# Output projection of the attention taken by halves of the positions, with the first half's norm inside it, and SBUF pools on two sides

## The chip, the cores and the metric

The kernel runs on one core of a Trainium2 chip. The metric is the device time of one execution in microseconds (us), lower is better; the median of three executions of the kernel before is 2689.87 us (2687.54 to 2693.98).

## The reference

A trunk of two layers over one sequence: S = 1024 positions, D = 1024 features, float32 throughout. The part that matters here is the end of layer 0's attention, its gated residual, and the start of the feed-forward network (FFN) behind it. `y` is the attention of all 16 heads times a sigmoid gate, before the output projection.

```python
# attention: 16 heads of 64, causal, a decay from a forget gate on the logits
    y = (att * sigmoid(o))                 # (S, D)
    x = x + g1 * (y @ w_out)               # output projection, gated residual
    h = rmsnorm(x, norm2_g) * (1 + sc2) + sh2
    a = h @ w_up                           # FFN up-projection, D x 5632
    a = causal_depthwise_conv3(a)          # over positions
    g, val = split(a)
    x = x + g2 * ((silu(g) * val) @ w_down)
```

Layer 1 replaces the attention by a spatial gating unit (SGU), and has an FFN too. `c` gives all shifts, scales and gates.

## The kernel before, in words

**Products.** A float32 product is made of three matmuls of halves: `pair` (L121) splits an operand into a rounded high part (a cast on ACT, L126) and the rest (a subtraction on DVE, L119), and `mm3` (called at L104) multiplies high by high, high by low and low by high. A "step" below is one such group of three 128x512 matmuls: one block of 128 features of `y` against one block of 128 output features, for a half (512) of the positions.

**Order.** All PE instructions of this part run in the order in which they are written (the chain in `mm`, as long as `inorder` is set). The order on DVE, ACT and on SP's DMA queue is made by a scheduler from the same program.

**The attention** goes through eight pairs of heads, p = 0 to 7. While the softmax of one pair keeps DVE and ACT busy, a second stream of work (`stream`) gives PE something to do: `tick(w)` takes steps from it at a rate (`rate`) per unit of attention work. For p = 1 to 7 the stream holds the input projection of the next pair. When the last projection is done, the stream goes on, at rate 1.4, with two things:

- `x_transposed`: the residual x is loaded (512 KB tiles), transposed by PE (16 groups of four 128x128 transposes, L157) and copied out of PSUM by ACT (L883) into eight tiles `xt[k, half]`, features on partitions;
- `out_early`: the output projection for pairs 0 to 5. For each of the eight output blocks m and both halves it makes the steps for p = 0 to 3, adds them to x with the gate (`axpy`, on DVE, L855), and then the same for p = 4 and 5. The operands `w` (blocks of w_out) and `y` are loaded as 256 KB pieces into a ring of two buffers `fraw` (L835) and split by `pair`.

**The tail.** When the attention has ended, the steps of p = 6 and 7 follow for both halves, 96 matmuls, and the last of these write the banks that the FFN will use (`bankX`, `bankY`).

**Between attention and FFN.** `arena` then opens the pool in which the FFN's operands live, on the memory that the attention's pools gave back. `operands1` makes the first operands from the first half of the positions: it writes x to DRAM (`spill`, L1108), squares it (ACT, L1085) and adds the squares (DVE, L1039) into one tile, sums that tile over the partitions with four one-column matmuls, takes the inverse root, spreads it over the partitions with a broadcast matmul (`norm_t`), multiplies (DVE, L1039) and modulates x (`scale`, ACT, L1073), and splits the result into high and low tiles `hc` (`put_op`; ACT L1026, DVE L1039). They are named B11 and B21 after the place they take in the FFN's blocked product. `square_half` (L1098) squares the second half, `start_up` loads and splits the FFN's first weights (`rw`, `ow`), and `next_operands` norms the second half within the FFN's first product, at hooks behind the 7th and 14th group of matmuls.

```python
                self.rate = 1.4
                yield from x_transposed()
                yield from out_early()
        ...
        self.fox()
        self.arena()
        s02 = self.ada_scale(0, 2)
        for _ in self.operands1(s02):
            pass
```

## Time and profile before

The profiled execution took 2692.37 us, 1.77 us of them outside the span of its engines.

| what | value |
|---|---|
| median of three runs | 2689.87 us |
| profiled execution, span | 2692.37 us, 2690.6 us |
| mean granted PE clock | 0.977 |
| PE busy, matmuls | 2563.3 us (95%), 12522 |
| DVE, ACT, POOL busy | 78%, 54%, 6% |
| attention's output projection begins in PE's stream | about 668 us |
| last matmul of the output projection issued | 802 us |
| first FFN matmuls in an unbroken row | from about 828 us |

How to read it: times are in us from the start of the span. A row of the timeline gives start, duration, engine, line, operation, output and inputs; in brackets stands how long the engine had been idle and which instruction on another engine released it. Matmuls overlap in the array, so the end of one row lies behind the start of the next; the distance between starts is what a matmul costs. "PEld" is the loading of a matmul's stationary operand. A row of the groups gives the busy time of all instructions of one form, the mean of one in ns, and the idle time ahead of them.

### The profile page before, as it was taken

To read this page: it belongs to the slowest core of one execution; us is meant where nothing else is said; L and a number is where in the kernel's file an instruction comes from. 1 tells how busy PE (TensorE), PEld (TensorE's weight loads), DVE (VectorE), ACT (ScalarE), POOL (GpSimd) and SP (SyncE) were. 2 spreads that over 40 slices of the span, in tenths; PEclk is the share of its full clock that TensorE was granted. 3 is DMA by queue.
4 is the path that set the end of the run, shared out by engine and by line. 5 is a ranking of instruction groups with operands and counts; after the bars stand their busy time and mean duration, and the time that the engine had idled before them with its cause. 6 is when DMAs were issued, how large, how long until landed. Compare 5 with 4: busy or idle time off the path is not lost.

```text
span 2690.6 us, 35246 instructions
## 1 busy us (share of the span) xinstructions
PE 2563.3 (95%) x12522; PEld 2179.0 (81%) x12522; DVE 2096.8 (78%) x3630; ACT 1458.9 (54%) x2310; POOL 173.7 (6%) x289
## 2 busy tenths in 40 slices
PE   6999999998997899999999999999998999999997
PEld 5988889898776688788888888888876888888886
DVE  7678777887768888898688766666888888877875
ACT  7347766777635454455446544654465555555444
POOL 1122222222200000000000000000000000000000
PEclk9999998998998999999999999999999999999999
DMA  6751111113222344545745346557452343337562
GB/s 232 245 172 56 56 54 54 56 52 118 74 85 62 115 128 149 170 137 198 252 159 178 98 154 194 186 180 278 157 174 73 102 149 114 118 102 287 161 197 90
DMA packets 315512, 377.61 MB, mean 140 GB/s; under 512 B 18760, under 2 KB 196040, under 8 KB 315336
## 3 DMA queue, kind: packets, MB, share of 16 engines
q1 hardware_dynamic: 315112, 375.30, 42.6%
q8 instruction: 98, 1.61, 0.2%
q14 instruction: 78, 0.64, 0.1%
q10 hardware_dynamic: 224, 0.06, 0.0%
HBM read 285.57 MB, written 89.72 MB: 139 GB/s over the span
## 4 chain that ended last, share of the span: by engine, by line
PE 80%; DVE 10%; ACT 5%; issue 2%; DMA 2%; POOL 0%; SPq 0%; DVEq 0%; ACTq 0%; POOLq 0%
PE bankX L104 20%; PE banka L104 18%; PE bankY L104 17%; PE pj L104 7%; PE ms L104 5%; PE o L104 3%; PE op L104 3%; PE s L104 2%; PE ms L157 2%; PE pv L104 2%; DVE hc L1039 1%; DVE ow L1039 1%; DVE x L1039 1%; PE ms L1645 1%; DVE x L1524 1%
## 5 line engine op out<-in xcount | busy, mean ns | idle before, releaser
L1026 ACT CAST ow<-rw 128x1024 fp32r<-128x1024 f32 (+1 forms) x438 | 398.7, 911 | 472.1 <-PE bankX L104 157.8
L1039 DVE TENSOR_TENSOR ow<-rw,ow 128x1024 fp32r<-128x1024 f32 (+1 forms) x438 | 457.9, 1046 | 172.7 <-ACT ow L1026 171.0
L104 PE MATMUL bankX<-hc,ow 128*128 128x512 f32 x1920 | 470.8, 393 | 18.0 <-DVE ow L1039 10.1
L104 PEld LDWEIGHTS bankX<-hc,ow 128*128 128x128 f32 x1920 | 361.2, 189 | 95.7 <-DVE ow L1039 11.6
L104 PE MATMUL banka<-hc,ow 128*128 128x512 f32 x1608 | 392.9, 393 | 6.5 <-ACT hc L1026 2.8
L104 PE MATMUL bankY<-hc,ow 128*128 128x512 f32 x1584 | 388.2, 392 | 0.8 <-DVE ow L1039 0.8
L104 PEld LDWEIGHTS banka<-hc,ow 128*128 128x128 f32 x1608 | 301.2, 189 | 71.3 <-ACT hc L1026 4.4
L104 PEld LDWEIGHTS bankY<-hc,ow 128*128 128x128 f32 x1584 | 296.0, 188 | 64.1 <-issue 1.9
L104 PE MATMUL pj<-x,h 128*128 128x384 f32 (+1 forms) x1536 | 315.5, 347 | 0.3 <-DVE x L119 0.3
L104 PEld LDWEIGHTS pj<-x,h 128*128 128x128 f32 x1536 | 271.3, 192 | 4.9 <-DVE x L119 0.5
L1524 DVE SCALAR_TENSOR_TENSOR x<-x,prm,x 128x1023 f32<-128x1023 f32 (+1 forms) x160 | 204.3, 1279 | 2.8 <-ACT x L1522 2.3
L104 PE MATMUL bankY<-ow 128*128 128x512 f32 x720 | 204.0, 391 | 0.2 <-DVE x L1043 0.2
L104 PE MATMUL banka<-ow 128*128 128x512 f32 x672 | 187.3, 391 | 0.5 <-DVE x L1043 0.5
L104 PEld LDWEIGHTS bankY<-ow 128*128 128x128 f32 x720 | 135.5, 189 | 28.7 <-DVE x L1043 0.6
L104 PE MATMUL bankX<-ow 128*128 128x512 f32 x588 | 156.1, 392 | 0.0
L104 PEld LDWEIGHTS banka<-ow 128*128 128x128 f32 x672 | 125.8, 188 | 27.3 <-ACT x L1073 0.9
L104 PE MATMUL ms<-ow 128*128 128x512 f32 x546 | 139.9, 390 | 0.9 <-DVE pp L1039 0.9
L104 PE MATMUL pv<-pt,w 128*128 128x256 f32 (+1 forms) x640 | 118.2, 293 | 14.0 <-ACT pt L782 11.4
L104 PEld LDWEIGHTS bankX<-ow 128*128 128x128 f32 x588 | 110.7, 188 | 23.5 <-issue 0.5
L119 DVE TENSOR_TENSOR pt<-ms,pt 128x512 fp32r<-128x512 f32 (+1 forms) x160 | 100.3, 632 | 29.6 <-ACT pt L782 28.1
L782 ACT CAST pt<-ms 128x512 fp32r<-128x512 f32 (+1 forms) x160 | 85.3, 539 | 67.3 <-PE ms L157 62.9
L104 PEld LDWEIGHTS ms<-ow 128*128 128x128 f32 x546 | 102.0, 188 | 23.7 <-DVE pp L1039 2.8
(293 smaller groups left out, 3884.8 us busy)
## 6 DMA issues: line engine op xcount, KB each, us to landing
rw<-yd SPq DMA_DIRECT2D x210, 256.0 KB
rw<-in_ffn_w_up_dram SPq DMA_DIRECT2D x88, 512.0 KB
yd<-pp SPq DMA_DIRECT2D x60, 512.0 KB
rw<-in_ada_w_dram SPq DMA_DIRECT2D x48, 512.0 KB
rw<-in_ffn_w_down_dram SPq DMA_DIRECT2D x88, 256.0 KB
rw<-in_sgu_w_in_dram SPq DMA_DIRECT2D x32, 512.0 KB
yd<-x SPq DMA_DIRECT2D x30, 512.0 KB
fraw<-in_fox_w_in_dram SPq DMA_DIRECT2D x96, 128.0 KB
```

The source lines that it names most:

```text
L104: i = self.nc.tensor.matmul(out, lhsT, rhs, start=start, stop=stop, skip_group_check=self.strict)
L119: return (eng or self.nc.vector).tensor_tensor(lo, full, hi.bitcast(F32), op=ALU.subtract)
L157: i = self.nc.tensor.transpose(ps[: s.shape[1], j * P : (j + 1) * P], s, self.ident)
L782: nc.scalar.copy(pt[:, 0, :nb], ps[:, :nb])
L1026: return self.ao(self.nc.scalar.copy(t[:, 0], src))
L1039: return self.vo(self.nc.vector.tensor_tensor(out, a, b, op=op))
L1524: stt(o[:, j:], a[:, : S - j], w[2 - j], o[:, j:], op0=ALU.mult, op1=ALU.add)
L1645: k = nc.tensor.matmul(px[:, b * P : (b + 1) * P], vn[:, b, c * P : (c + 1) * P], sg[:, 0], start=True, stop=True)
```

## The change

Seven things are done differently.

1. **Pools.** The pools of the attention (`shared`, `fox`) lie on the right side of SBUF; `qkv` and `fraw` are in a small pool `mid` on the left. When the attention ends, the right side is closed and the first tiles of the FFN (`arena_first`: hc 9 to 12, i.e. B11 and B21, the weight rings `rw` and `ow`, and scratch `pp`) are opened there while `mid` and the tiles of x and y live on.
2. **The stream by halves.** `out_first` replaces the earlier order: x of the first half of the positions only, then the projection of that half for pairs 0 to 6 in one accumulation per m (m = 4 to 7, then 0 to 3), while x of the second half is loaded and transposed in between. The rate is 1.9. The attention waits with the last values of pair 7's first half until this is complete.
3. **The first half's end.** `out_second` (rate 0.75) adds pair 7 for the first half, eight steps, each with its `axpy`. Behind each, ACT squares the finished block into a buffer of the ring `fraw`, and PE sums it over the partitions: four one-column matmuls for each of the eight blocks, accumulated, in place of the additions on DVE and a single such sum. Then follow the spill, the norm and the scaling of the first half, between the first steps of the second half (m = 0 to 2, pairs 0 to 6).
4. **Loads.** `out_raw` and its splits are queued in `back` and taken one at each tick. The blocks w of pairs 0 to 6 for m = 4 to 7 are loaded during the last input projection, their slots are then used for other things, and they are loaded and split a second time at the end: 37 pieces are split instead of 30.
5. **The tail.** After the attention come 129 matmuls: m = 3 of the second half for pairs 0 to 6 (21), pair 7 for m = 0 to 3 (12), and m = 4 to 7 whole (96). Between them the splits of B11 and B21 (`put_op`), the squares of the second half and the FFN's weight loads are issued.
6. **Banks.** The FFN's PSUM banks are opened at m = 5 of the tail, and the tail uses three of them (X0, X1, Y1).
7. **The start of the FFN.** `run` calls `arena` and `next_operands` right behind the tail; `operands1` is not called, nor is `square_half`.

The diff, cut to its core ("..." where lines are left out):

```diff
 PO = 3
-PC = 6
-LE = (1, 2)
+LO = 3
+LE = 5
...
-            self.sp = e2(tc.tile_pool(name="shared", bufs=1, reuse_waits="tile"))
-            fp = e2(tc.tile_pool(name="fox", bufs=1, reuse_waits="tile"))
+            mp = e2(tc.tile_pool(name="mid", bufs=1, reuse_waits="tile"))
+            es_r = es.enter_context(ExitStack())
+            self.sp = es_r.enter_context(tc.tile_pool(name="shared", bufs=1, side="right", reuse_waits="tile"))
+            fp = es_r.enter_context(tc.tile_pool(name="fox", bufs=1, side="right", reuse_waits="tile"))
...
-                return fp.tile(shape, dt, tag=tag, name=self.name(tag), bufs=bufs)
+                return (mp if tag in ("qkv", "fraw") else fp).tile(shape, dt, tag=tag, name=self.name(tag), bufs=bufs)
...
                     next(self.fill, None)
+                    if self.back:
+                        self.back.pop(0)()
...
-                    yield from proj(p, ws, rws[p], nw)
+                    yield from proj(p, ws, rws[p], nw, out_w1 if p == 7 else None)
                     ws = ws2
-                self.rate = 1.4
-                yield from x_transposed()
-                yield from out_early()
+                self.rate = 1.9
+                yield from out_first()
+                done.append(1)
+                while len(done) < 2:
+                    yield
+                self.rate = 0.75
+                yield from out_second()
...
+            def out_square(m, half):
+
+                if half and m == 0:
+                    self.acc = t = self.tile(self.tm, [P, 512], F32, "tm")
+                else:
+                    t = self.pp()[:, :512] if half else T([P, 512], F32, "fraw", 2)
+                nc.scalar.activation(t, self.xt[m % 4, half][:, m // 4 * 512 : (m // 4 + 1) * 512], AF.Square)
+                if half and m:
+                    self.tt(self.acc, self.acc, t, ALU.add)
+                return t
+
+            def out_sum(m, t):
+                if m == 0:
+                    self.acc = None, ps1("sq")
+                for b in range(4):
+                    self.mm(
+                        self.acc[1][:, b : b + 1],
+                        t[:, b * P : (b + 1) * P],
+                        self.ones[:, 0:1],
+                        m + b == 0,
+                        m + b == 10,
+                    )
+
...
+            def x_load(half):
+                more = self.wslot([P, 2, S], F32) if half else None
+                for i in range(4):
+                    t = more[:, i] if half and i < 2 else self.hslot(F32).rearrange("p a f -> p (a f)")
+                    d = nc.sync.dma_start(t, self.x[0, (4 * half + i) * P : (4 * half + i + 1) * P, :])
+                    if not (half and i < 2):
+                        self.chain("h", d)
+                    xs.append(t)
+
...
+            def out_w1():
+                out_w(range(7), 1)
+
+            def out_first():
                 self.xt = {(k, half): self.xslot([P, D]) for half in range(2) for k in range(4)}
...
+                x_load(0)
+                out_y(0)
+                out_w(range(2), 0)
+                for _ in range(3):
                     yield
+                yield from x_transposed(0)
+                xt = iter(())
+                for m in (4, 5, 6, 7, 0, 1, 2, 3):
+                    for i, _ in enumerate(out_mm(ps1("op"), range(7), m, 0)):
                         yield
+                        if i % 2:
+                            for _ in xt:
+                                yield
+                                break
+                    if m == 7:
+                        out_w(range(2, 7), 0)
+                        x_load(1)
+                        xt = x_transposed(1)
+                for _ in xt:
+                    yield
+                for n in range(2):
+                    out_w((7,), n)
+
+            def out_second():
+                out_y(1)
+                sq = {}
+                for m in range(KT):
+                    yield from out_mm(ps1("op"), range(7, 8), m, 0)
+                    sq[m] = out_square(m, 0)
+                    if m:
+                        out_sum(m - 1, sq[m - 1])
+                    yield
+                self.spill(0)
+                n = self.norm_t(0, *scales)
+                steps = [lambda: None, lambda: out_sum(7, sq[7]), lambda: next(n)]
+                steps += [lambda: None] * 7 + [lambda: next(n, None)]
+                steps += [lambda k=k, j=j: self.scale(k, j) for j in range(2) for k in range(4)]
+                for m in range(LO):
+                    open_ps[m] = ps1("op")
+                    for _ in out_mm(open_ps[m], range(7), m, 1, True, False):
+                        if steps:
+                            steps.pop(0)()
+                        yield
+                while steps:
+                    steps.pop(0)()
...
             flush()
             drain()
-            self.inorder = False
-            for i in range(2):
-                out_w(range(PC, 8), i)
-                out_y(range(PC, 8), i)
+            es_r.close()
+            self.arena_first()
+            for p in range(7):
+                del out["w", p, 1]
+            t3 = T([P, 3, 512], F32, "qkv", 3)
+            raws = [out_raw(w_src(p, 1), t3[:, p] if p < 3 else None) for p in range(5)]
+
+            def last_w(p):
+                raws.append(out_raw(w_src(p + 5, 1))) if p < 2 else None
+                out["w", p, 1] = self.pair(self.hslot(), raws[p], "h")
+
+            steps = [lambda: None] * 2
+            steps += [
+                lambda o=o, j=j, k=k: self.put_op(o, k, self.xt[k, 0][:, j * 512 : (j + 1) * 512])
+                for j, o in enumerate(("B11", "B21"))
+                for k in range(4)
+            ]
             banks = None
-            for half in range(2):
-                for m in range(KT):
-                    if (half, m) == LE:
-                        es_p.close()
-                        pp = self.ctx.enter_context(tc.tile_pool(name="banks", bufs=1, space=PSUM, reuse_waits="tile"))
-                        self.bank = {
-                            c: [pp.tile([P, 512], F32, name=f"bank{c}{i}") for i in range(2)] for c in "aXY"
-                        }
-                        banks = Ring(self.bank["X"] + self.bank["Y"])
-                    for _ in out_mm(banks() if banks else ps1("op"), range(PC, 8), m, half):
-                        pass
-
+            open_ps[LO] = ps1("op")
+            for p, _ in enumerate(out_mm(open_ps[LO], range(7), LO, 1, True, False)):
+                last_w(p)
+            for m in range(KT):
+                if m == LE:
+                    es_p.close()
+                    pp = self.ctx.enter_context(tc.tile_pool(name="banks", bufs=1, space=PSUM, reuse_waits="tile"))
+                    self.bank = {c: [pp.tile([P, 512], F32, name=f"bank{c}{i}") for i in range(2)] for c in "aXY"}
+                    banks = Ring([*self.bank["X"], self.bank["Y"][1]])
+                ps = open_ps.get(m) or (banks() if banks else ps1("op"))
+                for _ in out_mm(ps, range(7 if m <= LO else 0, 8), m, 1, m > LO):
+                    if steps:
+                        steps.pop(0)()
+                out_square(m, 1)
+                if m == 5:
+                    self.start_up(self.ffn_src(0), [lambda: None] * 4)
+        return scales
+
+
...
         nc, xt = self.nc, self.xt
         acc = self.acc
-        ps = self.tile(self.ms, [P, 512], F32, "ms")
-        for b in range(4):
+        if isinstance(acc, tuple):
+            acc, ps = acc
+        else:
+            ps = self.tile(self.ms, [P, 512], F32, "ms")
+        for b in range(4 if acc is not None else 0):
             i = self.mm(ps[:, b : b + 1], acc[:, b * P : (b + 1) * P], self.ones[:, 0:1], True, True)
...
-        self.fox()
+        scales = self.fox()
         self.arena()
-        s02 = self.ada_scale(0, 2)
-        for _ in self.operands1(s02):
-            pass
-        for j in (1, 0):
-            for k in range(4):
-                self.square_half(k, j)
-        self.start_up(self.ffn_src(0), [lambda: None] * 4)
-        self.next_operands(s02)
+        self.next_operands(scales)```

How instructions moved is seen at three places. In the names, `op` is a PSUM tile of the output projection; `qkv` and `h` are split pieces of y (behind the comma) or of w (behind the arrow); for pair 7 the y is `qkv`. `hc9` and `hc10` hold B11, `ow` an FFN weight.

PE, from the last steps of the output projection to the first matmuls of the FFN. Before, with the sum (`ms<-ones,pp`) and the broadcast (`ms<-tm,ones`) of the first half's norm between them:

```order
L104 MATMUL bankX1_9222<-qkv_1785_8916,h_1820_9127 128x512 x3
L104 MATMUL ms_1848_9316<-ones_77,pp0_9277 128x1 [waits DVE_49]
L104 MATMUL ms_1848_9316<-ones_77,pp0_9277 128x1 x3
L104 MATMUL ms_1854_9340<-tm_1853_9338,ones_77 128x512 [waits DVE_49]
L104 MATMUL banka0_9219<-hc9_1855_9350,ow0_9287 128x512 [waits Activation_49]
L104 MATMUL banka0_9219<-hc9_1855_9350,ow0_9287 128x512 [waits DVE_49]
```

After:

```order
L104 MATMUL bankY1_9324<-h_1771_8823,h_1841_9240 128x512 x3
L104 MATMUL bankY1_9324<-qkv_1803_8983,h_1728_8670 128x512 x3
L104 MATMUL banka0_9319<-hc9_1843_9258,ow0_9181 128x512 [waits PE_49,Activation_49]
L104 MATMUL banka0_9319<-hc9_1843_9258,ow0_9181 128x512
L104 MATMUL banka0_9319<-hc9_1843_9258,ow0_9181 128x512 [waits DVE_49]
L104 MATMUL banka0_9319<-hc9_1843_9258,ow0_9181 128x512 x3
```

The sum and the broadcast are no longer between the last step of the projection (`bankY1`) and the first of the FFN (`banka0`).

PE, pair 7 of the first half. Before, these steps stand between the last matmuls of the attention, with a y (`qkv_1673`) that was split at 763.24 us of the trace:

```order
L104 MATMUL op_1823_9135<-h_1816_9117,h_1812_9107 128x512 [waits DVE_49]
L104 MATMUL op_1823_9135<-h_1816_9117,h_1812_9107 128x512 x2
L104 MATMUL op_1823_9135<-qkv_1673_8350,h_1814_9112 128x512 x3
L104 MATMUL op_1824_9143<-h_1816_9117,h_1812_9107 128x512 [waits DVE_49]
L104 MATMUL pv_1793_8969<-pt_1805_9044,w_1592_8008 128x256 [waits Activation_49]
```

After, where `sq` is the PSUM tile of the sums of squares and `fraw` a squared block:

```order
L157 MATMUL ms_1788_8900<-ident_72,raw_1699_8502 128x128
L104 MATMUL op_1741_8720<-qkv_1677_8408,h_1726_8665 128x512 [waits Activation_49]
L104 MATMUL op_1747_8737<-qkv_1677_8408,h_1726_8665 128x512
L104 MATMUL op_1741_8720<-qkv_1677_8408,h_1726_8665 128x512 [waits DVE_49]
L104 MATMUL op_1741_8720<-qkv_1677_8408,h_1726_8665 128x512
L104 MATMUL op_1747_8737<-qkv_1677_8408,h_1726_8665 128x512 x2
L104 MATMUL sq_1753_8757<-ones_77,fraw_1744_8730 128x1 [waits Activation_49]
L104 MATMUL sq_1753_8757<-ones_77,fraw_1744_8730 128x1 x3
```

Pair 7's steps now wait for the cast and the subtraction of its y, and each finished block is followed by a sum of its square.

PE, a little later, where the first steps of the second half (`op_1800`) begin; y of the second half (`h_1759`, `h_1762`, `h_1771`: pairs 4, 5 and 6) comes through the ring `fraw`, as the squares do:

```order
L104 MATMUL op_1800_8953<-h_1759_8778,h_1673_8388 128x512 [waits Activation_49]
L104 MATMUL op_1800_8953<-h_1759_8778,h_1673_8388 128x512 [waits DVE_49]
L104 MATMUL op_1800_8953<-h_1762_8794,h_1675_8396 128x512 [waits Activation_49]
L104 MATMUL op_1800_8953<-h_1762_8794,h_1675_8396 128x512 [waits DVE_49]
L104 MATMUL sq_1753_8757<-ones_77,fraw_1773_8829 128x1 [waits Activation_49]
L104 MATMUL sq_1753_8757<-ones_77,fraw_1773_8829 128x1 x3
L104 MATMUL op_1800_8953<-h_1771_8823,h_1680_8422 128x512 [waits Activation_49]
L104 MATMUL sq_1753_8757<-ones_77,fraw_1777_8858 128x1 [waits Activation_49]
```

The sums of the later blocks stand behind steps that wait for a y of the same ring.

More of the change, by code (lines that the diff above doesn't have):

```diff
@@ L868, in x_transposed @@
[L868 to L887 removed]
+                if stop:
+                    self.axpy(self.xt[m % 4, half][:, m // 4 * 512 : (m // 4 + 1) * 512], t, gate[:, m : m + 1])
@@ L915, in fox @@
                     until(p + 1, 0)
+                else:
+                    flush()
+                    while not done:
+                        next(self.fill)
+                    done.append(1)
                 values(p, 2, 0, v)
@@ new lines, in fox @@
+            self.arena_first()
+            for p in range(7):
+                del out["w", p, 1]
[10 more added lines that the diff above has]
+            ]
```

108 lines of the change are left out of this document (49 added, 59 removed).

## The prediction

> **What bounds the kernel now.** I read the page first, then the windows of the stages around the change, then PE's waits there, and last the timeline.
>
> ```profile
> span 2690.6 us, 35246 instructions
> PE 2563.3 (95%) x12522; PEld 2179.0 (81%) x12522; DVE 2096.8 (78%) x3630; ACT 1458.9 (54%) x2310; POOL 173.7 (6%) x289
> ```
>
> PE is busy 95% of the span, so time can only be won where PE stands still or does avoidable work. The stages (columns: stretch and its length, busy time of PE, weight loads, DVE, ACT and POOL with counts, PE's granted clock, DMA share, GB/s):
>
> ```profile
> core 0: us, PE busy (x) PEld busy (x) DVE busy (x) ACT busy (x) POOL busy (x), PEclk, DMA share, GB/s
> 661.00:666.00 5.00, 2.66 (x12) 2.08 (x13) 4.97 (x13) 4.66 (x12) 3.12 (x6) 0.78 0.43 142
> 666.00:670.00 4.00, 4.00 (x20) 4.00 (x20) 3.26 (x14) 2.33 (x5) 0.08 (x1) 0.50 0.44 138
> 668.40:684.60 16.20, 13.13 (x81) 11.31 (x79) 12.26 (x39) 13.46 (x31) 4.78 (x8) 0.82 0.20 65
> 684.60:703.10 18.50, 16.11 (x93) 12.93 (x91) 12.62 (x29) 12.99 (x24) 3.48 (x5) 1.00 0.27 86
> 703.10:780.60 77.50, 77.50 (x409) 65.73 (x409) 57.14 (x117) 32.87 (x61) 7.00 (x10) 1.00 0.16 52
> 780.60:803.20 22.60, 22.53 (x99) 17.92 (x97) 12.91 (x20) 5.85 (x8) 0.00 (x0) 1.00 0.35 138
> 803.20:829.30 26.10, 5.91 (x14) 3.55 (x15) 23.16 (x41) 13.81 (x20) 0.00 (x0) 0.58 0.74 202
> 868.00:897.90 29.90, 20.87 (x78) 16.09 (x77) 29.57 (x37) 15.52 (x19) 0.00 (x0) 0.83 0.20 61
> ```
>
> From 703 to 803 us PE never stops: the steps of the output projection fill the attention's last pair. Between 803 and 829 us PE is busy 5.9 of 26.1 us, while DVE works 23.2. The stretch 868 to 898, where DVE is full and the second half is normed, has the same instructions in the same order in both kernels, so I leave it. PE's waits from 660 to 910 us (total, count, longest):
>
> ```profile
> PE ms L104 <- DVE pp L1039: 9.7, 1, 9.7
> PE ms L104 <- DVE tm L1039: 5.8, 1, 5.8
> PE ms L157 <- ACT x L883: 5.1, 8, 1.6
> PE banka L104 <- ACT hc L1026: 2.8, 1, 2.8
> ```
>
> The first, second and fourth are the norm of the first half: squares, sum, root, scaling, splits, one behind the other, with nothing else for PE. The third is the transposing of x, where PE waits for ACT's copies.
>
> ```profile
> 801.57 0.86 PE L104 MATMUL bankX<-h,h 128*128 128x512 f32 x3
> 802.27 0.86 PE L104 MATMUL bankX<-qkv,h 128*128 128x512 f32 x3
> 832.13 2.90 PE L104 MATMUL bankY<-hc,ow 128*128 128x512 f32 x12
> 834.65 1.08 PEld L104 LDWEIGHTS ms<-ones,hc 128*128 128x128 f32 x8
> 835.65 1.47 PEld L104 LDWEIGHTS banka<-hc,ow 128*128 128x128 f32 x7
> 840.59 1.02 PE L104 MATMUL ms<-tm,ones 128*128 128x512 f32 x2
> ```
>
> These give the prices. A step of three matmuls: 802.27 - 801.57 = 0.70 us, so 0.233 us each. A sum over the partitions: 835.65 - 834.65 = 1.00 us. A broadcast: about 1.0 us (1.02).
>
> **The change part by part.**
>
> *The empty stretch.* The last step ends at 802.27 + 0.70 = 802.97. Had the FFN's first twelve matmuls run without a wait, they would begin at 832.13 - 12 x 0.233 = 829.33. So 26.4 us are removed between them. One sum and one broadcast lie in it and are still needed elsewhere: net **-24.4 us**. This is a gain only if the FFN's first operands are ready when the last step ends; the tail gives PE 153 matmuls from the second half's fourth block (129) and the FFN's first 24, 35.7 us, and DVE has there, by the groups of 600 to 835 us here and below, 8 subtractions for B11 and B21 (0.69), 7 for w (0.72), 7 additions of squares (0.69, taken as the first), 8 `axpy` (0.75) and 8 subtractions for the FFN's weights (1.22): 31 us, so PE stays the longer of the two.
>
> ```profile
> L1039 DVE TENSOR_TENSOR ow<-rw,ow 128x1024 fp32r<-128x1024 f32 x4 | 4.8, 1220 | 0.0
> L1039 DVE TENSOR_TENSOR hc<-x,hc 128x512 fp32r<-128x512 f32 x8 | 5.1, 689 | 1.7 <-ACT hc L1026 1.7
> ```
>
> *The transposing of x.* The 5.1 us of waits (third row) were caused by 16 groups in a row. The change splits them by halves and places the second between steps: **-5.1 us**, and what replaces it is (a) below.
>
> *Sums on PE.* Eight sums stand where one stood: 7 x 1.00 = **+7.0 us**. Nothing hides them, PE being full there. DVE is relieved of the additions, which lie off the bound in that stage.
>
> *New waits.* The trace has none of these chains in this place, so I bound each by nearby rows, the groups of 600 to 835 us first (busy time in all, mean of one in ns, idle time before).
>
> ```profile
> L855 DVE SCALAR_TENSOR_TENSOR x<-op,mod,x 128x512 f32<-128x512 f32 x42 | 31.3, 749 | 15.2 <-PE op L104 14.9
> L119 DVE TENSOR_TENSOR h<-fraw,h 128x512 fp32r<-128x512 f32 x30 | 21.2, 717 | 9.7 <-ACT h L126 9.5
> L126 ACT CAST h<-fraw 128x512 fp32r<-128x512 f32 x30 | 18.3, 620 | 18.4 <-DMA fraw<-nat 7.7 <-PE op L104 4.3 <-PE ms L157 3.8
> L883 ACT COPY x<-ms 128x512 f32<-128x512 f32 x16 | 9.1, 582 | 3.3 <-PE ms L157 3.3
> L758 ACT ACTIVATE cv<-cv,smx 128x896 f32<-128x896 f32 x3 | 3.1, 1044 | 2.0 <-DVE smx L756 2.0
> L1073 ACT ACTIVATE x<-x,mod,a 128x512 f32<-128x512 f32 x8 | 6.2, 807 | 9.2 <-DVE x L1039 9.2
> L1098 ACT ACTIVATE hc<-x 128x512 f32<-128x512 f32 x8 | 4.6, 622 | 8.9 <-DVE x L855 8.8
> ```
>
> (a) The first half's 8 groups are still in a row, at a higher rate: half of 5.1, 2.5 us. The second half's x is loaded into slots that come free only after the block m = 7, and two y pieces go into slots that x gives up, with a cast and a subtraction (0.62 + 0.72) ahead of their steps: 1.7 + 1.3. Together 5.5, between 0 (all under the attention) and 8.
>
> (b) y of pair 7's first half. Before, other steps stood between it and its use; now it is used at once, behind a chain that the trace shows for the other half:
>
> ```profile
> 782.37 0.45 PE L104 MATMUL pv<-pt,w 128*128 128x256 f32 x3
> 784.83 0.41 ACT L126 CAST qkv<-so 128x256 fp32r<-128x256 f32 x1 [1.61 <-DVE so L801]
> 785.68 0.41 DVE L119 TENSOR_TENSOR qkv<-so,qkv 128x256 fp32r<-128x256 f32 x1
> ```
>
> From 782.37 to 785.68 + 0.41 are 3.7 us. In the new order ACT has casts and a softmax pass (1.04 us) ahead of this cast, so 4.3 us. PE has 15 transposes in between, 0.11 us apart:
>
> ```profile
> 659.91 0.27 PE L157 MATMUL ms<-ident,cv 128*128 128x128 f32 x1
> 660.02 0.27 PE L157 MATMUL ms<-ident,raw 128*128 128x128 f32 x1
> ```
>
> That covers 1.7 us; 2.6 us are lost, between 0 and 4.3. Queued behind on PE is all that is left of the attention.
>
> (c) The eight steps of pair 7 take 5.6 us and the seven sums between them 7.0; with 0.7 for the attention's matmuls PE has 13.3 us. DVE has eight `axpy` (6.0), seven subtractions for y of the second half (5.0), and the softmax's own work, for which I take 5.5 us: 0.4 of the stretch, below the 57.14 of 77.50 of the stage before it, which holds `axpy` and splits too. 16.5 against 13.3: 3.0 us, between 0 and 5.
>
> (d) A sum waits for its square: 0.62 us of ACT behind the `axpy`. Mostly later matmuls are in between; 1.2 us, between 0 and 2.
>
> (e) In the tail the casts of w (0.62) go between ACT's scalings (0.81); with the last y's chain and the opening of the banks at m = 5, 2.6 us, between 0 and 6.
>
> Losses together: 5.5 + 2.6 + 3.0 + 1.2 + 2.6 = **+15 us**, between 0 and 25.
>
> *Costed at nothing.* The seven extra pieces of w, seven casts and subtractions (9.4 us of two engines), lie under the tail's 35.7 us of PE; without this cover they would cost up to 5 us of DVE. The spills:
>
> ```profile
> 788.58 14.29 SPq L1108 DMA_DIRECT2D xd<-x  x7
> ```
>
> Seven issues in 14.3 us, about 2 us each; four of them now stand on SP's queue behind the y loads and ahead of w's, which have the rest of the attention to arrive. If not covered, 8 us.
>
> *Sum.* -24.4 - 5.1 + 7.0 + 15 = **-7.5 us** against the profiled 2692.4, thus 2684.9; that execution lies 2.5 us above the median, so about **2683 us** by the median. With all losses at 0 it is -22.5 (2667), with all at their upper end +2.5 (2692).
>
> *The clock.* After the stretch 661 to 666, where PE was busy 2.66 of 5.00 us, it had a clock of 0.50 for the next 4 us: half of 4 us is lost, 2 us. The Trainium skill, "TensorE: Matmul & The Clock Gate", section "What's actually happening", says the clock halves after an idle window of about 3.4 us and is full again after as long a busy one. By that rule the short waits above would cost no clock at all; the row shows the lower clock behind a stretch that was busy by half, so here the measurement decides, and it is a rival below.
>
> **The rivals.**
>
> *R1: the new chains are hidden.* In 703 to 780 PE had filler for every wait. If (a) to (e) find theirs too, and only some 5 us of the 15 are left: -24.4 - 5.1 + 7 + 5 = -17.5, **2672 us**. For it: that row of 77.50 of 77.50. Against it: the new order needs y and the sums right after they are made.
>
> *R2 (slower): the ring of two buffers decides.* Squares and y loads share `fraw`.
>
> ```profile
> 665.95 1.75 SPq L835 DMA_DIRECT2D fraw<-in_fox_w_out_dram  x2
> 668.99 0.62 ACT L126 CAST h<-fraw 128x512 fp32r<-128x512 f32 x1
> 670.64 0.69 DVE L119 TENSOR_TENSOR h<-fraw,h 128x512 fp32r<-128x512 f32 x1
> ```
>
> From issue (665.95) to the end of the subtraction (671.33) a load holds its buffer 5.4 us; I take 6. A square holds one from ACT's start to the end of its sum, 2.5 us if PE takes the sum at once. Seven loads and eight squares need (7 x 6 + 8 x 2.5)/2 = 31 us. PE's own work from the first of pair 7's steps to the last sum, counted by these prices, is about 31 us: at balance. But the later sums stand on PE behind steps that wait for a y of the same ring. If so each square holds its buffer about as long as a load, the need is 15 x 6/2 = 45 us, 14 us above PE's work: 2683 + 14 = **2697 us**. It decides once a square is held for more than some 4 us. Against it: the attention's own matmuls are there to be done meanwhile.
>
> *R3: half clock after new waits.* If (b) and the start of the tail each leave PE half idle, as at 661, 2 x 2 us more: **2687 us**. The skill's rule makes this 0; the row speaks for it.
>
> *R4: the FFN's first operands or weights are late*, since their memory on the right side is free only when the attention's last tiles are. Loads and splits then end behind the last step by some 5 us: **2688 us**. This would be the change not doing what it says in part.
>
> **How the numbers follow.** Forecast 0.42, with its own range 2678 to 2687 (about a third of the losses' spread either way); R1 0.20; R3 0.17; R2 0.15; R4 0.06. A measurement of this kernel can tell about 0.2%, 5.4 us, from no change: faster is below 2684.5, slower above 2695.3. Faster: 0.28 of the forecast, R1's 0.20, 0.04 of R3: 0.52. Slower: 0.14 of R2, 0.02 of the rest: 0.16. Same: 0.32. The range 2671 to 2695 leaves out the lower part of R1 and most of R2.
>
> **What would show it.** Right: the rows of PE waiting on `pp` and `tm` near 803 are gone and the first `banka` follows the last projection step within 2 us (else R4); 64 one-column records of `sq` at about 1 us per eight; one wait of 2 to 3 us on ACT or DVE `qkv` at pair 7's first step (b); waits on `axpy` within the eight steps (c) of about 3 us; the windows of the attention's last pair below 95% busy by some 10 us in all. R2 would show as PE waits on `h<-fraw` of the second half with SP's loads issued late, R3 as a clock of 0.50 in those windows, R1 as almost no waits before the tail. Wrong I would be if the FFN's first stages, or 868 to 898, changed their length, since nothing here counts them.

## The result

The changed kernel takes 2707.39 us (median of seven runs, 2700.8 to 2712.99) against 2693.98 us (seven runs, 2687.54 to 2695.67): a ratio of 1.0054, 95% interval 1.0038 to 1.0071. It is slower by about 13 us where 7 us faster was forecast. The profiled execution, 2712.99 us, is the slowest of the seven, 5.6 us above their median; its span lies 20.6 us above the one before.

The page of the changed kernel:

```profile
span 2711.2 us, 35378 instructions
PE 2597.6 (96%) x12578; PEld 2190.2 (81%) x12578; DVE 2082.7 (77%) x3609; ACT 1462.7 (54%) x2321; POOL 170.4 (6%) x289
```

PE is busy 34 us longer for 56 records more. To see where, I cut both executions at two instructions that both have: the last matmul of the last input projection (the 1536th `pj`), and the 25th `banka` matmul of the FFN. What lies between them is called the section here: it holds all that was moved. What follows has the same instructions in both; 80 of PE's 8187 stand in another order (at 1721 to 1757 us before). The windows of the section and of all that follows, before:

```profile
658.10:842.14 184.04, 155.63 (x789) 128.52 (x789) 134.15 (x286) 92.77 (x171) 18.46 (x28) 0.91 0.28 88
842.14:2690.60 1848.46, 1806.67 (x8187) 1492.74 (x8185) 1459.22 (x1970) 947.56 (x1298) 0.00 (x0) 0.99 0.48 157
```

and after:

```profile
659.44:840.13 180.69, 166.44 (x848) 137.92 (x847) 115.03 (x261) 96.24 (x180) 17.75 (x28) 0.92 0.33 108
840.13:2711.20 1871.07, 1830.69 (x8187) 1495.74 (x8185) 1462.88 (x1970) 946.67 (x1298) 0.00 (x0) 0.99 0.47 155
```

The section became shorter, 184.0 to 180.7 us. What follows became 22.6 us longer, and there PE is busy 24.0 us longer with exactly the same 8187 matmuls at the same clock (0.99). So single matmuls became slower. One stretch of the FFN's up-projection, where PE never waits, before (timeline of PE, one row per group of twelve):

```profile
917.17 2.88 PE L104 MATMUL bankX<-hc,ow 128*128 128x512 f32 x12
919.89 2.88 PE L104 MATMUL bankY<-hc,ow 128*128 128x512 f32 x12
925.33 2.88 PE L104 MATMUL banka<-hc,ow 128*128 128x512 f32 x12
928.05 2.20 PE L104 MATMUL bankY<-hc,ow 128*128 128x512 f32 x9
```

and after:

```profile
915.56 2.96 PE L104 MATMUL bankX<-hc,ow 128*128 128x512 f32 x12
918.36 2.96 PE L104 MATMUL bankY<-hc,ow 128*128 128x512 f32 x12
923.96 2.91 PE L104 MATMUL banka<-hc,ow 128*128 128x512 f32 x12
926.71 2.96 PE L104 MATMUL bankY<-hc,ow 128*128 128x512 f32 x12
```

From start to start a group takes 919.89 - 917.17 = 2.72 us before and 918.36 - 915.56 = 2.80 us after; `banka` 2.72 and 2.75. The groups from 900 us on (busy, mean of one in ns; `bankX<-ow` is `ow` with `ow`) show which matmuls are meant; before:

```profile
L104 PE MATMUL bankX<-hc,ow 128*128 128x512 f32 x1853 | 452.3, 392 | 9.4 <-DVE ow L1039 5.3 <-ACT ow L1026 3.9
L104 PE MATMUL bankX<-ow 128*128 128x512 f32 x588 | 156.1, 392 | 0.0
```

after:

```profile
L104 PE MATMUL bankX<-hc,ow 128*128 128x512 f32 x1848 | 460.2, 397 | 9.4 <-DVE ow L1144 5.6 <-ACT ow L1131 3.9
L104 PE MATMUL bankX<-ow 128*128 128x512 f32 x588 | 156.6, 393 | 0.2 <-DVE ow L1144 0.2
```

Products of `hc` (moving) with `ow` (stationary) are slower; `ow` with `ow` is not. What the change did to these is where they lie. The program's byte addresses within a partition:

```
                 before                    after
hc 9 to 12       43968 ...  (192 mod 256)  135136 ...  (224 mod 256)   right side
hc 13, 0 to 8    93120 ...  (192 mod 256)   43968 ...  (192 mod 256)   left side
ow 0 to 3       125888 ...  (192 mod 256)  184288 ...  (224 mod 256)   right side
```

The right side ends at 229344, 32 bytes below a multiple of 64, and its tiles are laid downward from there. After the change the weights `ow` lie 32 bytes off against hc 13 and 0 to 8, which feed most of `bankX` and `bankY` and a third of `banka`, and at the same place modulo 256 as hc 9 to 12 and as themselves. `ow` with `ow` is as fast at 224 as it was at 192, so it is not the place itself that goes with the speed. Pairing PE's records in order with the program's matmuls, I took the mean distance from one start to the next (those of 215 to 245 ns): 227 ns at the same place, 233.3 ns at 32 bytes off, for about 3400 matmuls seen in such a row: 3400 x 6.3 ns = 21 us. The program has 3528 of them, 22 us. The group of `banka` shown above is of hc 9 and 10, which agree with `ow`: its last six matmuls take 227 ns, its first six, behind a slow group, about 230. 528 matmuls of `banka` (hc 9 and 11) are like these six, 1.6 us together. That is about the 24 us of PE's busy time.

### The profile page after: what moved, and what is told of

Read it like the earlier page. It is cut to its first block, busy times and chain, and to the rows that moved or that the text cites. A ratio compares the mean times of both kernels' runs of the same rounds, so it can differ in the third digit from the quotient of the medians.

```text
span 2711.2 us, 35378 instructions
## 1 busy us (share of the span) xinstructions
PE 2597.6 (96%) x12578; PEld 2190.2 (81%) x12578; DVE 2082.7 (77%) x3609; ACT 1462.7 (54%) x2321; POOL 170.4 (6%) x289
## 4 chain that ended last, share of the span: by engine, by line
PE 80%; DVE 10%; ACT 4%; DMA 3%; issue 2%; SPq 0%; POOL 0%; DVEq 0%; ACTq 0%; POOLq 0%
PE bankX L104 20%; PE banka L104 18%; PE bankY L104 18%; PE pj L104 7%; PE ms L104 4%; PE o L104 3%; PE s L104 2%; PE ms L157 2%; PE op L104 2%; PE pv L104 2%; DVE ow L1144 1%; DVE hc L1144 1%; PE ms L1753 1%; DVE x L1144 1%; DVE x L1632 1%
## 5 line engine op out<-in xcount | busy, mean ns | idle before, releaser
L1131 ACT CAST ow<-rw 128x1024 fp32r<-128x1024 f32 (+1 forms) x438 | 398.1, 910 | 480.2 <-PE bankY L104 160.8
L1144 DVE TENSOR_TENSOR ow<-rw,ow 128x1024 fp32r<-128x1024 f32 (+1 forms) x438 | 457.6, 1046 | 182.0 <-ACT ow L1131 181.3
L104 PE MATMUL bankX<-hc,ow 128*128 128x512 f32 x1920 | 480.7, 399 | 17.8 <-DVE ow L1144 10.0
L104 PEld LDWEIGHTS bankX<-hc,ow 128*128 128x128 f32 x1920 | 361.5, 190 | 104.4 <-DVE ow L1144 11.9
L104 PE MATMUL banka<-hc,ow 128*128 128x512 f32 x1608 | 396.2, 395 | 1.1 <-DVE ow L1144 1.1
L104 PE MATMUL bankY<-hc,ow 128*128 128x512 f32 x1584 | 396.7, 398 | 0.0
L104 PEld LDWEIGHTS banka<-hc,ow 128*128 128x128 f32 x1608 | 301.4, 189 | 67.7 <-DVE ow L1144 1.4
L104 PEld LDWEIGHTS bankY<-hc,ow 128*128 128x128 f32 x1584 | 296.8, 188 | 70.6 <-issue 1.9
L104 PE MATMUL pj<-x,h 128*128 128x384 f32 (+1 forms) x1536 | 317.3, 349 | 0.2 <-DVE x L119 0.2
L104 PEld LDWEIGHTS pj<-x,h 128*128 128x128 f32 x1536 | 273.1, 194 | 5.0 <-DVE x L119 0.5
L104 PE MATMUL bankY<-ow 128*128 128x512 f32 x720 | 203.8, 391 | 0.2 <-DVE x L1148 0.2
L104 PE MATMUL banka<-ow 128*128 128x512 f32 x672 | 187.4, 392 | 0.5 <-DVE x L1148 0.5
L104 PEld LDWEIGHTS bankY<-ow 128*128 128x128 f32 x720 | 135.4, 189 | 28.5 <-DVE x L1148 0.6
L104 PE MATMUL bankX<-ow 128*128 128x512 f32 x588 | 156.6, 393 | 0.2 <-DVE ow L1144 0.2
L104 PEld LDWEIGHTS banka<-ow 128*128 128x128 f32 x672 | 125.9, 188 | 27.2 <-ACT x L1181 0.8
L104 PE MATMUL ms<-ow 128*128 128x512 f32 x546 | 140.0, 391 | 0.9 <-DVE pp L1144 0.9
L104 PE MATMUL pv<-pt,w 128*128 128x256 f32 (+1 forms) x640 | 119.1, 296 | 16.2 <-ACT pt L795 13.0
L119 DVE TENSOR_TENSOR pt<-ms,pt 128x512 fp32r<-128x512 f32 (+1 forms) x160 | 100.2, 632 | 41.6 <-ACT pt L795 39.8
L104 PEld LDWEIGHTS bankX<-ow 128*128 128x128 f32 x588 | 110.9, 189 | 24.2 <-issue 0.8
L104 PEld LDWEIGHTS ms<-ow 128*128 128x128 f32 x546 | 102.1, 188 | 23.7 <-DVE pp L1144 2.9
L795 ACT CAST pt<-ms 128x512 fp32r<-128x512 f32 (+1 forms) x160 | 85.2, 539 | 64.7 <-PE ms L157 55.1
```

Source lines behind the costliest of these rows:

```text
L104: i = self.nc.tensor.matmul(out, lhsT, rhs, start=start, stop=stop, skip_group_check=self.strict)
L119: return (eng or self.nc.vector).tensor_tensor(lo, full, hi.bitcast(F32), op=ALU.subtract)
L795: nc.scalar.copy(pt[:, 0, :nb], ps[:, :nb])
L1131: return self.ao(self.nc.scalar.copy(t[:, 0], src))
L1144: return self.vo(self.nc.vector.tensor_tensor(out, a, b, op=op))
```

## The experiments

**Is it the address?** One unused tile of 32 bytes is opened first on the right side. No instruction is added or moved.

```diff
+            pad = self.ctx.enter_context(tc.tile_pool(name="pad", bufs=1, side="right", reuse_waits="tile"))
+            pad.tile([P, 8], F32, name="pad0")
             es_r = es.enter_context(ExitStack())
```

> The changed kernel with one unused tile of 32 bytes opened first on the right side, so that everything there begins 32 bytes lower, at the same place modulo 128 as the tiles on the left; no instruction is added or moved. Theory A (a matmul is slower when its moving and its stationary operand lie at different offsets modulo some power of two): the groups of twelve bankX and bankY matmuls of the FFN go back from 2.80 to 2.72 us, the time falls by the 3402 slow matmuls x 6.4 ns = about 21.5 us, to 2686 where the changed kernel has 2707; the ratio to the kernel before is about 0.997. Rival B (the right side as such, or the distance of the two operands, or other engines' traffic makes them slow): groups stay at 2.80 us, time at 2707, ratio 1.005.

Measured: 2687.32 us, ratio to the kernel before 0.998 (0.997 to 0.999). All `hc` with `ow` matmuls are at 227 ns again. A stretch of the timeline, and the windows of the section and of what follows:

```profile
916.22 2.88 PE L104 MATMUL bankY<-hc,ow 128*128 128x512 f32 x12
918.94 2.88 PE L104 MATMUL bankX<-hc,ow 128*128 128x512 f32 x12
```

```profile
660.87:839.10 178.23, 164.69 (x847) 136.55 (x847) 114.98 (x261) 95.95 (x180) 17.75 (x28) 0.93 0.33 110
839.10:2686.90 1847.80, 1805.08 (x8187) 1491.08 (x8185) 1458.19 (x1970) 947.17 (x1298) 0.00 (x0) 0.99 0.48 157
```

2.72 us a group, and what follows the section takes 1847.8 us, as before (1848.5). 32 bytes that nobody uses give back 20 us of the time: theory A holds, and the right side as such is not the cause. The same in the other direction, in the kernel before:

```diff
+        ap.tile([P, 8], F32, name="pad0")
         self.rawr = ring("rw", 4, [P, S])
         self.owr = ring("ow", 4, [P, 2, S], F32R)
+        ap.tile([P, 8], F32, name="pad1")
```

> The kernel before with 32 unused bytes ahead of its rings rw and ow and 32 behind them: the FFN's weights move by 32 bytes against the hc tiles, nothing else moves and no instruction changes. Theory A: all 5112 hc<-ow matmuls (bankX 1920, banka 1608, bankY 1584) take 0.2333 instead of 0.2269 us, 33 us more, 2690 to 2694 becomes about 2725; groups of twelve take 2.80 us in all three banks; ow<-ow matmuls stay at 0.227. Rival B: no difference from the kernel before, ratio 1.000.

Measured: 2719.3 us, ratio 1.0106 (1.009 to 1.0122).

```profile
910.02 2.96 PE L104 MATMUL bankX<-hc,ow 128*128 128x512 f32 x12
912.82 2.95 PE L104 MATMUL banka<-hc,ow 128*128 128x512 f32 x12
915.61 2.96 PE L104 MATMUL bankX<-hc,ow 128*128 128x512 f32 x12
```

```profile
839.78:2714.90 1875.12, 1835.40 (x8187) 1491.61 (x8185) 1463.97 (x1970) 946.88 (x1298) 0.00 (x0) 0.99 0.47 154
```

All three banks are slow now, and PE is busy 28.7 us longer behind the section; the kernel lost 26 us of the 33 expected. Some 2 us were hidden where PE waits anyway (idle 41.8 us before, 39.7 now); the other 4 us the runs don't account for.

**Which offsets count?** Four single runs with other pads (96 bytes on the right side; 128 and 96 around `rw` and `ow` in the kernel before; and 256 ahead of them), the diffs as above with other sizes.

> The changed kernel with 96 unused bytes first on the right side: moving and stationary operand of bankX and bankY then lie 64 bytes apart modulo 128, instead of 32. If the difference that counts is taken modulo 64, matmuls go back to 0.227 us and the time is about 2686; if it is taken modulo 128 or more, they stay at about 0.2333 and the time at about 2707. Rival B (other causes): 0.2333 too, so this run decides only together with the first.

> The kernel before with 128 unused bytes ahead of rw and ow and 128 behind: weights 128 bytes from the hc tiles modulo 256. If the difference counts modulo 128, the groups of twelve stay at 2.72 us and the time at 2690 to 2694; if modulo 256 or more, they take 2.80 us and the time is about 2725.

> The kernel before with 256 unused bytes ahead of rw and ow and none behind: the weights then lie 256 bytes off, modulo 1024, from hc 9 to 13 and hc 0, and at the same place as hc 1 to 8. If only the difference modulo 256 counts, all groups stay at 0.227 us a matmul and the time at 2690 to 2694. If it counts modulo 512 or more, banka and part of bankX and bankY take up to 0.2333 us, and the time rises by some 15 us.

> The kernel before with 96 unused bytes ahead of rw and ow and 96 behind: the weights lie 96 bytes behind hc 9 to 13 and hc 0, and 96 ahead of hc 1 to 8, modulo 256. Offsets of 32 either way gave 233.3 ns a matmul, 64 gave 229.6, 128 gave 232.5, 0 and 256 gave 227. If the cost goes with how few powers of two the offset holds, 96 gives 233 and the time about 2719; if 0 is only one of several good offsets, 96 gives 227.

```
moving against stationary,   mean distance   time, one run (kernel)
bytes modulo 256             of starts, ns
  0                          227             2692.4 (before, 256 bytes; 0 as well)
 32 either way               233.3           2719.3 (before, median of four)
 64                          229.4 to 230.5  2701.3 (changed kernel)
 96 either way               233.3 to 234.0  2723.2 (before)
128                          232.5           2718.3 (before)
```

The 64 bytes fit neither of the two values expected: the cost is a third to a half of the others'. 128 bytes cost, so a match modulo 128 is not enough; 256 bytes cost nothing, so modulo 256 is. 96 bytes cost what 32 do; that the cost goes with the powers of two in the offset is not borne out, since 128 cost nearly as much as 32 and 64 less.

One thing more stands in these traces: a matmul whose own operands agree can be slow beside others whose operands don't. Besides the six of `banka` above, the run with 64 bytes has 229.8 ns for hc 9 to 12, which agree there. And in the kernel before, the last steps of the output projection (0.70 us for three, in the prediction) take 233 ns a matmul: `qkv` lies 64 bytes off against its `h`, and the `h` with `h` steps between them agree and are as slow. In the padded kernel both agree and both take 227. How far behind a slow matmul this reaches was not tested. Which part of the chip makes it so the traces don't say. The Trainium skill, "SBUF — State Buffer", section "A bandwidth-pool intuition that's wrong (but worth ruling out)", gives TensorE a second, independent read port for the weights; by that alone the two addresses would not matter to each other. In these runs they matter, by 6.3 ns a matmul at 32 bytes, and the measurement decides.

**What bounds the section, once the address is mended?** Three changes to the padded kernel, each alone. First, the squares of the first half are added on DVE and summed once on PE:

```diff
-                if half and m == 0:
+                if m == 0:
...
-                if half and m:
+                if m:
                     self.tt(self.acc, self.acc, t, ALU.add)
...
-                    sq[m] = out_square(m, 0)
-                    if m:
-                        out_sum(m - 1, sq[m - 1])
+                    out_square(m, 0)
```

> The changed kernel with the 32 unused bytes, and the first half's squares added on DVE into one tile as before, so that one sum on PE stands in place of eight. From PE's 1536th pj matmul to the FFN's 25th banka matmul the padded kernel has 178.2 us, 164.7 of them busy and 13.5 idle. Theory: PE bounds this section and the seven sums were 7.0 us of it: busy falls to about 157.7, idle stays within 1.5 us, the section takes 171 to 172.5 us and the kernel 2680 to 2681, 0.25% under the padded one. Rival: DVE sets the pace around pair 7's eight steps; the seven additions (4.8 us) then come back as idle time, and the section takes 176 us or more.

Measured: 2683.09 us, ratio to the kernel before 0.9963 (0.9951 to 0.9976).

```profile
660.45:832.33 171.88, 155.51 (x792) 127.02 (x792) 118.66 (x268) 96.06 (x180) 18.24 (x28) 0.96 0.34 114
```

The section fell by 6.4 us, PE's busy time by 9.2; idle time rose by 2.8 us. About half of the 9.2 is clock: by the record of the granted clock PE did 11.2 us of its work in this section at half clock, where the padded kernel did 20.5, so 4.6 us less are lost. The rest is PE's time for the sums, as the theory had it, and a part came back as waits. That DVE sets the pace, as the rival has it, is not shown: the largest new wait is for a softmax on ACT, which stood behind other work of ACT.

```profile
PE ms L157 <- ACT raw L777: 2.7, 1, 2.7
```

Second, the squares in tiles of their own:

```diff
-                    t = self.pp()[:, :512] if half else T([P, 512], F32, "fraw", 2)
+                    t = self.pp()[:, :512] if half else self.tile(self.tm, [P, 512], F32, "tm")
```

> The padded kernel with the first half's squares in the tiles tm, no longer in the ring fraw that the y loads use. Rival R2 of the prediction (the ring of two decides): the waits of the second half's first steps on h (0.23, 0.88, 0.23 us at 767 to 771 in the changed kernel) and the wait of sq go, and with them 3 us or more of the section's 13.5 us idle. Theory: the ring was not at its limit; the section stays within 1.5 us of 178.2.

Measured: 2687.18 us, ratio 0.9978 (0.9968 to 0.9987): the time of the padded kernel. The section's idle time went from 13.5 to 12.9 us. The waits on `h` at 769 to 772 us went, as the rival has it, but in the padded kernel they were 0.45 us, and the wait of `sq` stayed (1.0 us). In this profile the section was 174.0 us, which the theory did not allow: two half-clock stretches of 3.4 us fewer fell into it. The median did not follow. The ring of two was not the bound.

Third, `self.rate = 1.4` in `out_first` in place of 1.9:

> The padded kernel with rate 1.4 in place of 1.9 for the first half's steps, so that some are left to be done in one row ahead of the last values of pair 7's first half. Theory (step b: PE stood idle there because its filler was used up): the waits of 0.47, 0.93 and 2.20 us at 740 to 746 us and the half clock of 6.83 us behind them go, 3.6 + 3.4 = 7 us, and 171 to 173 us are left of the section's 178.2; the kernel 0.2 to 0.25% under the padded one. Rival: the softmax of pair 7 then ends later against PE, and the same waits turn up after the row or earlier for want of filler; the section stays at 177 to 180.

Measured: 2683.35 us, ratio 0.9963 (0.995 to 0.9975). The waits ahead of pair 7's steps went; the tail has others:

```profile
793.33 1.22 PE L104 MATMUL op<-h,h 128*128 128x512 f32 x2 [3.46 <-ACT h L126]
797.55 0.80 PE L104 MATMUL op<-h,h 128*128 128x512 f32 x1 [3.00 <-DVE h L119]
```

```profile
656.92:829.84 172.92, 160.90 (x848) 134.55 (x847) 113.81 (x261) 95.23 (x180) 17.67 (x28) 0.94 0.34 113
```

172.9 us, within the 171 to 173 expected; the kernel gained 4 us, 0.15%, a little less than the 0.2 to 0.25% expected. The first and the third change lead to the combination, and to one more attempt on the tail's waits:

> The padded kernel with both: the first half's squares added on DVE with one sum on PE, and rate 1.4 for the first half's steps. Apart they gave -0.17% and -0.17% of the time against the padded kernel (2683.1 and 2683.4 against 2687.3). If the two gains have different causes (PE's sums, and PE standing idle ahead of pair 7's steps) they add: about 2679, ratio to the kernel before 0.995. If both only shift the same wait, which in the rate 1.4 kernel stands at the last w pieces (3.46 and 3.00 us at 793 to 798 us), the second adds nothing: 2683.

Measured: 2670.12 us, ratio **0.9914** (0.9901 to 0.9928), faster than both kernels.

```profile
659.83:821.74 161.91, 152.58 (x792) 126.67 (x791) 117.82 (x268) 96.10 (x180) 17.67 (x28) 0.97 0.36 121
```

The section falls from 178.2 to 161.9 us, 16.3 us, where the two alone gave 6.4 and 5.3. The surplus is idle time: 9.3 us here, against 16.4 with one sum alone and 12.0 with the rate alone. One half-clock stretch is left, with 9.0 us of PE's work in it where the padded kernel had 20.5 in four. The tail's waits of 3.46 and 3.00 us are two of 0.99 us here; the runs don't show why. In the last run the last two w pieces of the tail go into tiles `pp`:

```diff
-            raws = [out_raw(w_src(p, 1), t3[:, p] if p < 3 else None) for p in range(5)]
+            raws = [
+                out_raw(w_src(p, 1), t3[:, p] if p < 3 else None if p < 5 else self.pp()[:, :512]) for p in range(7)
+            ]
```

> The same, with the last two of the seven w pieces of the tail loaded into tiles pp instead of the ring fraw, so that all seven loads can be issued ahead of the FFN's weight loads. Theory: the waits on h of 3.46 and 3.00 us in the tail come from these two loads sharing the DMA engines with seven of 512 KB; they go, and the time falls by up to 6.5 us, to 2673 to 2676. Rival: splitting them (cast and subtraction, 1.3 us apiece) is what is late; the time stays where the run without it is.

Measured: 2678.58 us, ratio 0.9948 (0.9935 to 0.9962): 8 us slower than without it, so neither the theory nor the rival. SP's queue, without `pp` (the combination) and with it:

```profile
762.85 17.80 SPq L853 DMA_DIRECT2D fraw<-in_fox_w_out_dram  x4
```

```profile
757.99 1.12 SPq L853 DMA_DIRECT2D fraw<-in_fox_w_out_dram  x2
759.20 18.21 SPq L853 DMA_DIRECT2D pp<-in_fox_w_out_dram  x2
777.47 23.33 SPq L1293 DMA_DIRECT2D rw<-in_ffn_w_up_dram  x8
```

Both rows end with the last `w` load, 120.8 us behind the section's start without `pp` and 121.9 with it. So only one of the two loads went ahead, and the last one did not. That `pp` lies where tiles of the attention still live is my reading of it. The row of 18 us is not what makes the difference, since the ring has one as long. PE waits longer for the split of these pieces, without `pp` and with it:

```profile
786.96 1.19 PE L104 MATMUL op<-h,h 128*128 128x512 f32 x4 [0.99 <-DVE h L119]
```

```profile
793.87 2.07 PE L104 MATMUL op<-h,h 128*128 128x512 f32 x4 [4.87 <-DVE h L119]
```

Why the split comes later there, and whether the loads compete with `rw`, is open.

## Why the prediction was wrong, point by point

**The step that failed** is what the working took for granted behind the section: it leaves the stretch from 868 us because it "has the same instructions in the same order in both kernels", and counts nothing for the FFN's stages. The same instructions were taken to cost the same time. The pools on the other side got no term; they were treated as a matter of when memory comes free (R4), never of where it lies. The profiles put +22.6 us in its place, from operands of `hc` and `ow` 32 bytes apart modulo 256, and the run with the pad took 20 us of the time back. The prediction's last sentence named the only way in which it would show, the FFN's stages changing their length, and this is what happened; no rival was made of it. (The sum itself comes to 2682 by the median rather than 2683; nothing hangs on it.)

**Inside the section** the working can be held against the traces term by term (us):

```
term                          forecast   changed   padded
empty stretch 803 to 829        -24.4     -24.4     -24.4   its rows are gone
waits of the x transposes        -5.1      -5.1      -5.1
seven more sums                  +7.0      +6.1      +6.1   eight took 7.0 and 6.9, start to next start
new waits, (a) to (e)           +15       +11.1     +10.4   idle 14.2 and 13.5, less 3.1 as before
half clock outside the stretch    0        +7.5      +5.9
sum                              -7.5      -4.8      -7.1
section, measured                         -3.4      -5.8
```

The first two terms stand as forecast in all columns, and 1.3 to 1.4 us stay open in both measured ones.

The empty stretch went as described. The last projection step and the FFN's first matmuls stand in one row:

```profile
826.71 0.85 PE L104 MATMUL bankY<-qkv,h 128*128 128x512 f32 x3
827.39 2.91 PE L104 MATMUL banka<-hc,ow 128*128 128x512 f32 x12
```

So R4 was wrong too: nothing was late. The new waits in the changed kernel's section (total, count, longest):

```profile
PE ms L157 <- DVE pt L119: 3.3, 3, 2.2
PE op L104 <- ACT h L126: 2.8, 2, 2.0
PE pv L104 <- ACT pt L795: 2.3, 2, 2.1
PE ms L157 <- DMA h<-in_x_dram: 1.6, 2, 0.8
PE pv L104 <- DVE pt L119: 1.4, 2, 0.9
PE op L104 <- DVE h L119: 0.7, 3, 0.3
PE sq L104 <- ACT fraw L886: 0.7, 1, 0.7
```

- (a), 5.5 us: 2.5, most of it (1.6) x of the second half arriving late, as described; (d), 1.2: 0.7; (e), 2.6: 2.4, at the last y and w in the tail. Right in kind, a little high.
- (b), 2.6 us: 3.6, but not where it was put. At pair 7's first step PE does not wait for `qkv` (the one wait for it, 0.2 us at 804 us, is in the tail). The filler is used up earlier, and PE waits for the softmax's `pt` ahead of the step:

```profile
740.55 0.57 PE L104 MATMUL pv<-pt,w 128*128 128x256 f32 x3 [0.47 <-DVE pt L119]
742.51 0.55 PE L157 MATMUL ms<-ident,cv 128*128 128x128 f32 x3 [0.93 <-DVE pt L119]
745.26 1.97 PE L157 MATMUL ms<-ident,raw 128*128 128x128 f32 x8 [2.20 <-DVE pt L119]
```

  The run at rate 1.4 removed these waits and won 4 us; that confirms the cause.
- (c), 3.0 us: nothing. No step of the eight waits for an `axpy`.
- R2: the loads of y through the ring cost 1.3 us at 767 to 771 us, not 14, and other buffers changed nothing in the time.
- R3, half clock after new waits: right, and larger than its 4 us. The clock record of the changed kernel has stretches of half clock at 709, 744, 771 and 805 us, each within 3.4 us behind such a wait; R3 had named those at 744 and 805. The window from 740 to 752 us:

```profile
740.00:752.00 12.00, 7.75 (x36) 6.00 (x36) 7.67 (x18) 6.43 (x12) 3.15 (x6) 0.72 0.11 33
```

PE did 23.8 us of its busy time in the section at half clock, 16.5 before; half of each is lost, 11.9 against 8.3, and 3.9 us of the latter lay in the stretch that was removed.

With the address mended, the change does about what was forecast: 5.6 us less than before where 7 were said. That the size comes so close is in part luck: the new waits were put 4.6 us too high, and the half clock, 5.9 us, was left out of the sum and to a rival. The forecast's mechanism and sign hold for the section; for the kernel they fall to a term that was not there.

## What to carry to other kernels

When a change moves operand tiles, compare the byte addresses of moving and stationary tiles modulo 256, and pad until they agree: here the difference is 20 us on 3528 matmuls and 26 us on 5112, at no instruction. This was tried with one form alone, 128x128 by 128x512 in float32r. In the profile it shows as a longer distance between starts in rows without any wait, at an unchanged count and clock. And a wait of 1 us on PE costs more than its length when a stretch of half clock follows it: here filler that lasts (rate 1.4) was worth 4 us more than filler that comes early (1.9).

## What was not expected of the hardware

A float32r matmul of 128x128 by 128x512, `hc` with `ow` in an unbroken row, takes 227 ns when moving and stationary operand start at the same address modulo 256 bytes, and 229.4 to 234 ns when they are 32, 64, 96 or 128 bytes apart. Some that agree take 229 to 233 ns beside others that don't.

In the record of the granted clock the half-clock stretches of the section last 3.41, 6.83 or 10.24 us, so the clock changes in steps of 3.41 us. In the changed kernel's section half clock set in after steps in which PE had stood idle for 1.2 us (before 770.8 us) to 2.2 us (before 804.9 us), so well short of a whole idle one. The share of idle time does not settle it alone: a step with 1.6 us idle (from 385.1 us) left the clock full, and in the padded kernel half clock set in after one with 0.45 us (before 772.1 us).

Two edits that were worth 4 us each alone gave 17 us together. In the section the surplus is idle time; why the one edit's waits went with the other is not shown.
